# The sums of the MLP's first weight blocks move from VectorE to GpSimd

## The chip, the cores and the metric

The kernel runs on one core of one Trainium2 chip. The metric is device time in microseconds (us). The engines are named as in the profile: PE is TensorE, DVE is VectorE, ACT is ScalarE, POOL is GpSimd, SP is SyncE, which issues the loads.

## The reference

A two-layer decoder trunk over 512 positions of width 1024. Layer 0 mixes with a gated MLP over chunks and with latent attention, layer 1 with gated linear attention. Each layer ends with the same MLP of width 4096, and that is where the change lies:

```python
def sqrelu_mlp(x, w1, w2):
    return jnp.square(jax.nn.relu(x @ w1)) @ w2

x = layer_norm(ALPHA * x + y, ln1_g[layer], ln1_b[layer])
x = layer_norm(ALPHA * x + sqrelu_mlp(x, w_ff1[layer], w_ff2[layer]), ln2_g[layer], ln2_b[layer])
```

## The kernel before

All products are made in fp32 quality from three products of reduced precision: each operand is split into a high part (a cast on ACT, L164) and a low part, the operand less its high part (a subtraction on DVE, L165). For a weight block the parts are the tiles `whi` and `wlo`, for an activation `hh` and `hl`. PE multiplies high by high, high by low and low by high.

The MLP, `ff`, treats `x @ w1` in eight groups of columns. A group takes 256 columns of the left half of `w1` and 256 of the right half; together with the two halves of the rows that makes four blocks of 512 x 256: B11, B12, B21, B22. Group 0 is multiplied plainly. Groups 1 to 7 go by a Strassen-like scheme with seven products instead of eight, `P1, p5, p7, p6, p3, P2, p4` in this order (`LATER`, L506). These need seven weight blocks: B11, B21 and B22 as loaded, and four sums, made in place:

- t1 = B11 + B12 (over B11), used by p5
- t3 = B12 + B22 (over B12), used by p7
- t2 = t1 + B22 (over t1), used by p6
- t4 = t2 + B21 (over t2), used by p4

A sum may begin when both its inputs are there and when the block that it overwrites has been split. `SUM` (L353) holds this table.

The order of the weight blocks is the list `wseq`: in a group B11, t1, t3, t2, B22, B21, t4. Between groups stand the blocks of the second matrix, ("w2", chunk, half, row half). After group 0 come the w2 products of chunk 0, then groups 1 and 2 one behind the other, then chunk 1, group 3, chunk 2, group 4 and so on, so that groups 1 and 2 have no w2 products between them. `upto(n)` (L533) walks that list: it issues loads up to six blocks ahead and calls `terms1` (a block of `w1`) or `terms2` (a block of `w2`), each of which splits a block. It is called ahead of each product with the place of the block that the product needs, plus a few blocks of lead.

Three things set the order of work. PE and DVE run their instructions in the order in which the program writes them (`manual_schedule` for PE, `in_order` for DVE in the MLP). ACT, POOL and SP get an order from the framework's planner. Semaphores are put in by the framework wherever a tile is written and read by different engines.

Before the change `sum1` (L369) puts a sum on DVE (L374). `upto` calls it for the block about to be split and, one step early, for the next block in the list if that is a sum other than t1 (L543 to L546). So sums and low parts stand in one queue on DVE.

After a product, `product` (L455) joins accumulators and makes the squared ReLU: V and X (L489, L490), then the quarters C11, C22 (L477), C12 (L481), C21 (L485); each quarter goes through two ACT instructions (L428, L429), a cast to `hh` on ACT and a low part `hl` on DVE.

Raw blocks lie in the tiles `cr` (two buffers for B11 and B12 of one group) and `cr2` (one buffer with room for B22 and B21).

Of the kernel before, what the change touches and what calls it, by code (L numbers as in the profile page):

```python
# [17 lines left out]
ALU = mybir.AluOpType  # L18
# [85 lines left out]
def trunk(ctx: ExitStack, tc: tile.TileContext, a: dict, out: bass.AP):  # L104
    nc = tc.nc
# [57 lines left out]
    def split(hi, lo, src):  # L163
        nc.scalar.copy(hi, src)  # L164
        nc.vector.tensor_tensor(lo, src, hi.bitcast(F32), ALU.subtract)  # L165
# [19 lines left out]
    def tb(t):  # L185
        return slice(t * P, (t + 1) * P)
# [97 lines left out]
    def ff(layer, hp, fp, xp, out_proj, prefetch):  # L284

        w1, w2 = a["w_ff1"][layer], a["w_ff2"][layer]
# [64 lines left out]
        raws, got_w, kept2 = {}, {}, {}  # L351
        BLOCK = {"B11": (0, 0), "B12": (0, 1), "B22": (1, 1), "B21": (1, 0)}
        SUM = {"t1": ("B11", "B12"), "t3": ("B12", "B22"), "t2": ("t1", "B22"), "t4": ("t2", "B21")}  # L353

        def load1(g, n):

            for m in (n,) if g == 0 else {"B11": ("B11", "B12"), "B21": ("B21",), "t1": ("B22",)}.get(n, ()):
                if g == 0 and m != "B22":
                    raw = wp.tile([P, WG], F32, tag="raw", name="raw", bufs=3)
                elif g == 0 or m in ("B11", "B12"):  # L360
                    raw = xp.tile([P, WG], F32, tag="cr", name="cr", bufs=2)
                else:
                    if g not in kept2:
                        kept2[g] = xp.tile([P, 2, WG], F32, tag="xk", name="cr2")
                    raw = kept2[g][:, m == "B21"]
                raws[g, m] = raw
                nc.sync.dma_start(raw.rearrange("p (k c) -> p k c", k=HK_), w1v(*BLOCK[m], g))

        def sum1(g, n):  # L369

            if n in SUM and (g, n) not in raws:
                x, y = SUM[n]
                raws[g, n] = raws[g, x]
                nc.vector.tensor_tensor(raws[g, n], raws[g, x], raws[g, y], ALU.add)  # L374

        def pair(spare=None):

            if spare is not None:
                return [xp.tile([P, WG], F32R, tag=t, name="ws", **({"bufs": 2} if t == "cr" else {})) for t in spare]
            return wp.tile([P, WG], F32R, tag="whi", name="whi"), wp.tile([P, WG], F32R, tag="wlo", name="wlo")  # L380
# [3 lines left out]
        LAST = [("s4h", "s4l"), ("s3h", "s3l"), ("s2h", "s2l"), ("cr", "cr")]  # L384

        def terms1(g, n):
            sum1(g, n)
            raw = raws[g, n]
            if (g, n) == (0, "B22"):
                his = [hp.tile([P, HK_, P], F32R, tag="hh", name="wh") for _ in range(2)]  # L390
                los = [hp.tile([P, HK_, P], F32R, tag="hl", name="wl") for _ in range(2)]
                for j in range(2):
                    split(his[j], los[j], raw.rearrange("p (k c) -> p k c", k=HK_)[:, :, tb(j)])
            else:
                hi, lo = pair(EARLY[n] if g == 0 else None)
                split(hi, lo, raw)
                his, los = ([z.rearrange("p (k c) -> p k c", k=HK_)[:, :, tb(j)] for j in range(2)] for z in (hi, lo))
            got_w[g, n] = his, los

        def load2(c, n, half):  # L400
            r = half * 2048 + c * GF
            raw = wp.tile([P, WG], F32, tag="raw", name="raw", bufs=3)
            nc.sync.dma_start(raw.rearrange("p (k c) -> p k c", k=2),
                              w2[r:r + GF, n * 512:(n + 1) * 512].rearrange("(k p) c -> p k c", p=P))
            raws["w2", c, n, half] = raw

        def terms2(c, n, half):
            raw = raws.pop(("w2", c, n, half))
            hi, lo = pair(LAST[(c - NG + 2) * 2 + half] if c >= NG - 2 and n == 1 else None)
            split(hi, lo, raw)  # L410
            v = lambda x: x.rearrange("p (k c) -> p k c", k=2)
            got_w["w2", c, n, half] = v(hi), v(lo)
# [94 lines left out]
        slots, wseq = [], []  # L507
# [22 lines left out]
        at = {"load": 0, "terms": 0}  # L530
        LOADS, TERMS = 6, 6

        def upto(n, loads=None):  # L533

            while at["load"] < min(len(wseq), n + (LOADS if loads is None else loads)):
                w = wseq[at["load"]]
                at["load"] += 1
                (load2(*w[1:]) if w[0] == "w2" else load1(*w))
            while at["terms"] < min(len(wseq), n):
                w = wseq[at["terms"]]  # L540
                i = at["terms"]
                at["terms"] += 1
                if w[0] != "w2":  # L543
                    sum1(*w)
                if i + 1 < at["load"] and wseq[i + 1][1] in SUM and wseq[i + 1] != (w[0], "t1"):
                    sum1(*wseq[i + 1])  # L546
                (terms2(*w[1:]) if w[0] == "w2" else terms1(*w))

        todo = 0
        for _ in out_proj:  # L550
            todo += 1
            upto(min(todo, 4), 2)
        sums = x_sums()
        for n, (i, j, k) in enumerate(itertools.product(range(2), repeat=3)):
            upto(min(8, 4 + max(0, n - 1)))
            if n in (4, 5):
                next(sums)
            plain(i, j, k)
            if n == 1:
                x_T(NT - 1)  # L560
                x_lo(NT - 2)
                x_lo(NT - 1)
        for i, s in enumerate(slots):
            if s[0] == "w2":
                need = max(place["w2", s[1], s[2], 1], place["w2", s[1], s[2], 0])
                if s[1] == 0:
                    next(sums, None)
                    upto(max(need + 1, 8 + i // 2))
                else:
                    upto(min(need + 1 + TERMS, need + 1 + 2 * (s[3] + 1)))  # L570
                ff2_half(s[1], s[2], s[3])
                continue
            upto(place[s[0], PRODUCTS[s[1]][1]] + 1 + min(TERMS, 2 + s[0]))
            product(*s)
# [718 lines left out]
    with (tc.tile_pool(name="h0", bufs=8) as hp, tc.tile_pool(name="f0", bufs=2) as fp,  # L1293
          tc.tile_pool(name="x0", bufs=1) as xp, in_order()):
        v0 = ff(0, hp, fp, xp, steps, load_v0)
    with tc.tile_pool(name="m1", bufs=1) as mp:
        steps = out_proj_odd(odd_mixer(mp, v0))
    with (tc.tile_pool(name="h1", bufs=8) as hp, tc.tile_pool(name="f1", bufs=2) as fp,
          tc.tile_pool(name="x1", bufs=1) as xp, in_order()):
        ff(1, hp, fp, xp, steps, None)  # L1300
# [38 lines left out]
```

## Time and profile before

| | us |
|---|---|
| median of 3 runs | 1174.79 (1174.71 to 1175.62) |
| the profiled execution | 1176.24 |
| its span | 1174.2 |
| PE busy | 1146.1 (98%) |
| DVE busy | 825.3 (70%) |
| ACT busy | 520.3 (44%) |
| POOL busy | 4.6 (0%) |

The span is what the trace covers; 2.0 us of the profiled execution lie outside it. Matmuls overlap and their ends are modelled, so a busy PE is one that is not kept waiting. The MLP of layer 0 lies at about 231 to 550 us, that of layer 1 at about 822 to 1170 us.

### The profile page before, as it was taken

How to read it: one execution, taken by the hardware profiler on the slowest of the kernel's cores; microseconds unless marked ns; L12 is line 12 of the kernel's file. 1: busy time of each engine (PE TensorE's matmuls, PEld its weight loads, DVE VectorE, ACT ScalarE, POOL GpSimd, SP SyncE). 2: the span in 40 equal slices, each digit the busy share in tenths (PEclk: the TensorE clock that was granted, in tenths of full speed). 3: DMA queues.
4: the chain of work that ended last, by engine and by line, in shares of the span. 5: the costliest groups of instructions: out<-in, count | busy, mean ns of one | idle time of the engine just before them, and what ended most of it. 6: DMA issues, size and time to landing. Idle time of an engine off the chain costs nothing.

```text
span 1174.2 us, 17121 instructions
## 1 busy us (share of the span) xinstructions
PE 1146.1 (98%) x6888; PEld 999.5 (85%) x6888; DVE 825.3 (70%) x1562; ACT 520.3 (44%) x801; POOL 4.6 (0%) x13
## 2 busy tenths in 40 slices
PE   8999999999899999999999999999998999999997
PEld 8988788889888998997888888778998889889976
DVE  5745687785677567568758559898766866675665
ACT  5367462443644534443264433443536444445430
POOL 0000000000000000000000000000000000000000
PEclk9999999999999999999999999999999999999999
DMA  7413143132341332214235312221232333413121
GB/s 243 148 37 108 55 137 97 36 109 72 108 141 57 127 126 76 86 55 157 72 97 144 90 54 73 72 72 55 77 104 90 111 105 109 142 38 126 54 90 54
DMA packets 84206, 111.67 MB, mean 95 GB/s; under 512 B 6080, under 2 KB 53056, under 8 KB 84128
## 3 DMA queue, kind: packets, MB, share of 16 engines
q1 hardware_dynamic: 84128, 110.59, 29.6%
q8 instruction: 54, 0.88, 0.3%
q14 instruction: 24, 0.20, 0.1%
HBM read 108.47 MB, written 2.10 MB: 94 GB/s over the span
## 4 chain that ended last, share of the span: by engine, by line
PE 86%; DVE 7%; ACT 5%; issue 1%; DMA 0%; SPq 0%; DVEq 0%; ACTq 0%
PE f L443 24%; PE f L160 9%; PE f L161 9%; PE f L159 9%; PE vg L159 3%; PE vg L161 3%; PE vg L160 3%; PE op L159 3%; PE op L161 2%; PE op L160 2%; PE sc L822 1%; PE qk L159 1%; DVE wlo L165 1%; PE qk L160 1%; PE qk L161 1%; PE o L844 1%
## 5 line engine op out<-in xcount | busy, mean ns | idle before, releaser
L164 ACT CAST whi<-cr 128x1024 fp32r<-128x1024 f32 x98 | 99.9, 1047 | 179.4 <-DVE cr L374 116.8
L160 PE MATMUL f<-wlo,hh 128*128 128x512 f32 x448 | 177.0, 395 | 1.5 <-DVE wlo L165 1.5
L161 PE MATMUL f<-whi,hl 128*128 128x512 f32 x448 | 177.0, 395 | 0.5 <-DVE hl L165 0.5
L159 PE MATMUL f<-whi,hh 128*128 128x512 f32 x448 | 176.8, 395 | 0.0
L165 DVE TENSOR_TENSOR wlo<-cr,whi 128x1024 fp32r<-128x1024 f32 x98 | 118.8, 1219 | 15.0 <-ACT whi L164 14.9
L443 PE MATMUL f<-XH,wlo 128*128 128x256 f32 x448 | 126.1, 281 | 1.6 <-DVE wlo L165 1.6
L443 PE MATMUL f<-XH,whi 128*128 128x256 f32 x448 | 126.1, 281 | 0.8 <-ACT whi L164 0.8
L443 PE MATMUL f<-XL,whi 128*128 128x256 f32 x448 | 125.8, 281 | 0.0
L165 DVE TENSOR_TENSOR hl<-r,hh 128x512 fp32r<-128x512 f32 x64 | 44.2, 690 | 109.8 <-ACT hh L164 109.8
L160 PEld LDWEIGHTS f<-wlo,hh 128*128 128x128 f32 x448 | 84.3, 188 | 21.5 <-DVE wlo L165 2.4
L161 PEld LDWEIGHTS f<-whi,hl 128*128 128x128 f32 x448 | 84.3, 188 | 21.1 <-DVE hl L165 1.4
L159 PEld LDWEIGHTS f<-whi,hh 128*128 128x128 f32 x448 | 84.3, 188 | 19.2
L443 PE MATMUL f<-sh,wlo 128*128 128x256 f32 x336 | 96.2, 286 | 4.5 <-DVE wlo L165 4.5
L443 PE MATMUL f<-sh,whi 128*128 128x256 f32 x336 | 95.8, 285 | 0.0
L443 PE MATMUL f<-sl,whi 128*128 128x256 f32 x336 | 95.8, 285 | 0.0
L208 DVE SCALAR_TENSOR_TENSOR XN<-XN,f 128x512 f32<-128x512 f32 (+1 forms) x113 | 73.4, 676 | 20.1 <-PE f L161 20.1
L443 PEld LDWEIGHTS f<-XH,wlo 128*128 128x128 f32 x448 | 84.4, 188 | 2.0 <-DVE wlo L165 2.0
L443 PEld LDWEIGHTS f<-XH,whi 128*128 128x128 f32 x448 | 84.4, 188 | 1.8 <-ACT whi L164 1.2
L443 PEld LDWEIGHTS f<-XL,whi 128*128 128x128 f32 x448 | 84.4, 188 | 0.5
L164 ACT CAST whi<-raw 128x1024 fp32r<-128x1024 f32 x56 | 58.5, 1051 | 54.6 <-PE f L443 38.3
L137 ACT CAST whi<-raw 128x1024 fp32r<-128x1024 f32 (+3 forms) x61 | 60.2, 991 | 50.0 <-DMA raw<-in_w_in_odd 22.1
L138 DVE TENSOR_TENSOR wlo<-raw,whi 128x1024 fp32r<-128x1024 f32 (+3 forms) x61 | 69.9, 1151 | 15.2 <-ACT whi L137 15.0
(270 smaller groups left out, 2536.7 us busy)
## 6 DMA issues: line engine op xcount, KB each, us to landing
raw<-in_w_ff SPq DMA_DIRECT2D x70, 512.0 KB, 4.2
cr<-in_w_ff SPq DMA_DIRECT2D x58, 512.0 KB, 4.3
raw<-in_w_in_odd SPq DMA_DIRECT2D x24, 512.0 KB, 4.2
XN<-in_x SPq DMA_DIRECT2D x16, 256.0 KB, 3.3
raw<-in_w_in_even SPq DMA_DIRECT2D x8, 512.0 KB, 3.9
raw<-in_w_out_even SPq DMA_DIRECT2D x8, 512.0 KB, 3.7
raw<-in_w_out_odd SPq DMA_DIRECT2D x8, 512.0 KB, 3.5
LB<-in_ln_b SPq DMA_DIRECT2D x4, 512.0 KB, 4.3
```

The costliest lines, as they stand in the source:

```text
L137: nc.scalar.copy(hi[:, :n], raw[:, :n])
L138: nc.vector.tensor_tensor(lo[:, :n], raw[:, :n], hi[:, :n].bitcast(F32), ALU.subtract)
L159: nc.tensor.matmul(acc, lh, rh, start=first, stop=False)
L160: nc.tensor.matmul(acc, lh, rl, start=False, stop=False)
L161: nc.tensor.matmul(acc, ll, rh, start=False, stop=last)
L164: nc.scalar.copy(hi, src)
L165: nc.vector.tensor_tensor(lo, src, hi.bitcast(F32), ALU.subtract)
L208: nc.vector.scalar_tensor_tensor(x, x, ALPHA if first else 1.0, acc, ALU.mult, ALU.add)
L443: nc.tensor.matmul(d, l, r, start=first and j == k == i == 0, stop=j == 1 and k == HK_ - 1 and i == 2, skip_group_check=True)
L822: nc.tensor.matmul(sc[:, :N], qts[t][:B_QK, h, :], KT[:, h, :N], start=True, stop=True)
L844: nc.tensor.matmul(os[t][:, h, :], pT[:, j * P:(j + 1) * P], V[:, j, h, :], start=j == 0, stop=j == t)
```

## The change

`sum1` and its calls in `upto` go. In its place `sums1(g)` is called after each block of a group g > 0 has been split. It goes through the table of sums and issues, on POOL, each sum whose inputs have been loaded or made, if the block that it overwrites has been split (t3 is the exception: it overwrites B12, which is never split, and waits only for t1 to be issued, which reads B12). So t1 and t3 are written behind the split of B11, t2 behind that of t1, t4 behind that of t2.

```diff
-        def sum1(g, n):
-
-            if n in SUM and (g, n) not in raws:
-                x, y = SUM[n]
-                raws[g, n] = raws[g, x]
-                nc.vector.tensor_tensor(raws[g, n], raws[g, x], raws[g, y], ALU.add)
+        made = set()
+
+        def sums1(g):
+
+            for n, (x, y) in SUM.items():
+                if (g, n) not in raws and (g, x) in raws and (g, y) in raws and (n == "t3" or (g, x) in made):
+                    if n == "t3" and (g, "t1") not in raws:
+                        continue
+                    raws[g, n] = raws[g, x]
+                    nc.gpsimd.tensor_tensor(raws[g, n], raws[g, x], raws[g, y], ALU.add)
...
         def terms1(g, n):
-            sum1(g, n)
             raw = raws[g, n]
+            made.add((g, n))
...
             got_w[g, n] = his, los
+            if g:
+                sums1(g)
...
                 w = wseq[at["terms"]]
-                i = at["terms"]
                 at["terms"] += 1
-                if w[0] != "w2":
-                    sum1(*w)
-                if i + 1 < at["load"] and wseq[i + 1][1] in SUM and wseq[i + 1] != (w[0], "t1"):
-                    sum1(*wseq[i + 1])
                 (terms2(*w[1:]) if w[0] == "w2" else terms1(*w))
```

## Rows read from the trace of the kernel before

**Rows 1.** The page's first part: busy time, share of the span, instructions.

```profile
PE 1146.1 (98%) x6888; PEld 999.5 (85%) x6888; DVE 825.3 (70%) x1562; ACT 520.3 (44%) x801; POOL 4.6 (0%) x13
```

**Rows 2.** Windows: length, busy time of each engine, PEclk (granted clock), DMA share.

```profile
302.00:304.00 2.00, 0.12 (x1) 0.12 (x2) 2.00 (x3) 0.00 (x0) 0.00 (x0) 1.00 0.00 0
304.00:306.00 2.00, 2.00 (x12) 2.00 (x13) 2.00 (x2) 0.00 (x0) 0.00 (x0) 0.62 0.00 0
306.00:308.00 2.00, 2.00 (x12) 2.00 (x12) 2.00 (x3) 1.88 (x2) 0.00 (x0) 0.52 0.00 0
...
340.00:382.00 42.00, 42.00 (x265) 37.81 (x264) 30.37 (x35) 19.81 (x25) 0.00 (x0) 1.00 0.31 101
```

**Rows 3.** Timeline of PE: start, length, instruction; in brackets the wait before it.

```profile
294.33 0.39 PE L443 MATMUL f<-XH,whi 128*128 128x256 f32 x1 [0.42 <-ACT whi L164]
295.64 0.39 PE L443 MATMUL f<-XH,wlo 128*128 128x256 f32 x1 [0.81 <-DVE wlo L165]
303.88 0.39 PE L443 MATMUL f<-sh,wlo 128*128 128x256 f32 x1 [2.25 <-DVE wlo L165]
...
330.36 0.50 PE L160 MATMUL f<-wlo,hh 128*128 128x512 f32 x1 [0.73 <-DVE wlo L165]
...
895.27 0.58 PE L443 MATMUL f<-sh,wlo 128*128 128x256 f32 x1 [2.26 <-DVE wlo L165]
```

**Rows 4.** Timeline of DVE around group 2 of layer 0.

```profile
287.35 1.22 DVE L165 TENSOR_TENSOR wlo<-cr,whi 128x1024 fp32r<-128x1024 f32 x1
...
291.37 0.69 DVE L165 TENSOR_TENSOR hl<-r,hh 128x512 fp32r<-128x512 f32 x1 [2.19 <-ACT hh L164]
291.98 1.22 DVE L374 TENSOR_TENSOR cr<-cr 128x1024 f32<-128x1024 f32 x1
293.23 1.23 DVE L374 TENSOR_TENSOR cr<-cr,cr 128x1024 f32<-128x1024 f32 x1
294.37 1.22 DVE L165 TENSOR_TENSOR wlo<-cr,whi 128x1024 fp32r<-128x1024 f32 x1
...
297.24 1.22 DVE L165 TENSOR_TENSOR wlo<-cr,whi 128x1024 fp32r<-128x1024 f32 x1
298.38 0.69 DVE L485 TENSOR_TENSOR f<-f,LG 128x512 f32<-128x512 f32 x1
302.00 0.69 DVE L165 TENSOR_TENSOR hl<-r,hh 128x512 fp32r<-128x512 f32 x1 [2.93 <-ACT hh L164]
302.61 2.35 DVE L165 TENSOR_TENSOR wlo<-cr,whi 128x1024 fp32r<-128x1024 f32 x2
...
326.74 0.69 DVE L165 TENSOR_TENSOR hl<-r,hh 128x512 fp32r<-128x512 f32 x1 [1.98 <-ACT hh L164]
```

**Rows 5.** Timeline of ACT in the same stretch.

```profile
290.71 1.14 ACT L164 CAST hh<-r 128x512 fp32r<-128x512 f32 x2
293.23 1.05 ACT L164 CAST whi<-cr 128x1024 fp32r<-128x1024 f32 x1 [1.37 <-DVE cr L374]
...
297.36 2.00 ACT L164 CAST whi<-cr 128x1024 fp32r<-128x1024 f32 x2 [1.66 <-DVE cr L374]
...
299.75 1.04 ACT L164 CAST whi<-cr 128x1024 fp32r<-128x1024 f32 x1
```

**Rows 6.** Groups by line: the larger group of sums (count, busy us, mean ns).

```profile
L374 DVE TENSOR_TENSOR cr<-cr,cr 128x1024 f32<-128x1024 f32 x42 | 51.1, 1217 | 0.1
```

**Rows 7.** Timelines of POOL and DVE, 25 to 30 us.

```profile
25.16 0.40 POOL L777 COPY kn<-kr 128x256 f32<-128x256 f32 x1 [24.65 <-DVE ny L182]
27.98 0.68 POOL L896 TENSOR_SCALAR_AFFINE_SELECT ws<-ws 128x512 f32<-128x512 f32 x1 [2.42 <-DMA ws<-in_a_w_s]
...
25.87 0.94 DVE L138 TENSOR_TENSOR wlo<-raw,whi 128x768 fp32r<-128x768 f32 x1
...
28.27 1.20 DVE L138 TENSOR_TENSOR wlo<-raw,whi 128x768 fp32r<-128x768 f32 x1
```

**Rows 8.** Timeline of SP's queue, 277 to 286 us: loads of blocks of `w1`.

```profile
277.68 0.92 SPq L367 DMA_DIRECT2D cr<-in_w_ff  x2
```

## The prediction

> **What bounds the kernel now.** I read the busy shares first, then TensorE's waits, then the granted clock in slices of 2 us around the longest wait, then the queues of VectorE (DVE) and ScalarE (ACT) in order of time. TensorE is busy 98% of the span, DVE 70%, GpSimd (POOL) 0% [rows 1]. So DVE's 825 us are not the bound, and taking work off DVE pays only where TensorE stands still for it. In the steady part of the MLP it never does: from 340 to 382 us TensorE is busy for all 42 us and DVE for 30 [rows 2]. What is left are a few gaps. In layer 0 the product p5 of group 2 waits 0.42 us for the high part of its block t1 and 0.81 us for the low part, p6 of group 2 waits 2.25 us for the low part of t2, and the first w2 product that needs block (1, 1, 1) waits 0.73 us; the second layer repeats them (2.26 us for the long one) [rows 3]. After the 2.25 us gap the granted clock reads 0.62 and 0.52 for two slices of 2 us, where it was 1.00 before; the 1.23 us of the two gaps before it cost no clock [rows 2, 3]. 0.62 and 0.52 of 2.4 GHz lie between its two levels, so most of these 4 us ran at 1.2 GHz: (0.38 + 0.48) x 2 = 1.7 us lost. Shorter gaps at the close of a layer lie behind group 7, where no sum is left to make, and stay.
>
> That gives a ceiling: 0.42 + 0.81 + 2.25 + 0.73 + 1.7 = 5.9 us a layer, 11.8 us for both. The change cannot bring more than about 1%.
>
> **Why the long gap is there.** Groups 1 and 2 follow each other with no w2 products between them, so DVE must prepare seven blocks while TensorE uses seven. Its queue there, in the written order [rows 4]: low part of B11 (287.35), a wait for ACT until hl at 291.37, the sums t1 and t3 of group 2 (291.98, 293.23), low t1 (294.37), a sum, low t3 (297.24), the subtraction of C21 (298.38), 2.93 us of waiting for ACT, hl (302.00), low t2 (302.61). TensorE resumes 1.27 us after the start of the last, at 303.88. ACT's side [rows 5]: the cast of t1 waits 1.37 us for its sum, that of t2 1.66 us, and a cast slips into the chain of C21: the same chain without one makes DVE wait 1.98 us (326.74) instead of 2.93 [rows 4].
>
> **The change, part by part.** *Removed from DVE:* 2 layers x 7 groups x 4 = 56 sums of 1.217 us (42 of them in one group of rows), 68.2 us [rows 6]. Hidden behind TensorE everywhere but in the gaps above, so worth nothing by itself.
>
> *Added to POOL:* 56 sums of 128x1024 f32. No row shows this operation. The nearest are a copy of 256 columns (0.40 us) and a select over 512 columns (0.68 us), each with one input [rows 7]. Their difference gives 0.28 us for 256 columns, 1.09 ns a column, and 0.12 us fixed. A sum reads two inputs: 0.12 + 1024 x 1.09 ns = 1.2 us if the second input is free (as on DVE, 1.22 us), 2.35 us if each column is paid twice. An engine that takes 0.40 us for 256 copied columns is no faster with more inputs, so I take the upper end, 2.4 us, and keep 1.2 to 4.5 us for the range. In a sentence by itself: the Trainium skill, GPSIMD Engine Reference, section 3.1, has 4497 ns for a sum of 2048 columns; half of that, 2.25 us, would give the same sum within 0.2 us.
>
> *Beside it, DVE loses time.* Two subtractions of 128x768 with both inputs in SBUF stand in the trace, one that began after the copy had ended (0.94 us) and one of which 0.39 us lay beside the select (28.27 to 28.66): it took 1.20 us [rows 7]. So 0.26 of 0.39 us were lost, two thirds of the time shared. All low parts (`wlo`, `hl`) are of this kind; the subtractions that read PSUM I take as free. One case only, and with a one-input operation: I keep zero and full loss as the ends and take two thirds. The Trainium skill's GPSIMD Engine Reference, section 1, says the same kind of thing, that the engine shares its SBUF interfaces with VectorE and conflicts with instructions of two SBUF inputs; the row agrees (0.26 us lost), and what it would make of the time is the second rival.
>
> *Order and queues.* POOL's queue holds nothing else in the MLP. A group's sums stand in it as t1, t3, t2, t4; t3 needs the load of B22 and would hold t2 back if that came late. No DMA is moved; the load of a next block still waits for the low parts that read the old one. What is new is that ACT's cast waits for POOL, not for DVE; behind that cast stand the casts and Relu's of the other group, and behind them DVE's low parts in written order.
>
> *The stretch again, group 2 of layer 0.* Low B11 ends at 288.5 as before. POOL makes t1 from 288.6 to 291.0, t3 to 293.4. ACT's two casts `hh` end at 291.85, then its cast of t1 takes 1.05 us, to 292.9 (it began at 293.23 before). hl (291.37) loses 0.4 us beside t3, low t1 starts at 292.9, loses 0.3 and ends at 294.4. TensorE reaches p5 at 293.9 and needs the low part two matmuls later: a gap of some 0.3 instead of 1.23 us. POOL makes t2 from 294.4 to 296.8. The other hl (0.61 us) loses 0.4 beside it and ends at 295.4. Low t3 then has 1.4 us beside t2, does 0.47 of its 1.13 us in that time and the rest by 297.5; it ended at 298.38. From there it is C21's chain as before: in the trace TensorE resumed 298.38 + 5.50 = 303.88; without the cast inside the chain it is 2.93 - 1.98 = 0.95 shorter. So TensorE resumes between 297.5 + 4.55 = 302.05 and 297.5 + 5.50 = 303.0. Which of the two is ACT's order, which no line of the kernel writes; I take the middle, 302.5: **1.4 us gained**, between 0.9 and 1.8.
>
> *The clock.* From 295.64 to 301.63 TensorE took 6.0 us to get from the second gap to the long one; now it starts at 294.4, loses some 0.3 at t3, and arrives at 300.7. The new gap is 1.4 to 2.3 us, against 2.25 that cost clock and 1.23 that did not. I take half of the 1.7 us, **0.9**, between 0 and 1.7.
>
> *The 0.73 us gap.* One sum (t1 of group 3, 1.13 us) leaves DVE's queue ahead of that block, but POOL then makes t1 and t3 of group 3 just there, beside an hl and the low part waited for: (0.61 + 1.13) us of work could lose more than the sum gave. I take 0, between +0.7 and -1.0, and a loss of 0.2 for t4, whose sum now starts only when low t2 is done.
>
> Sum: 1.4 + 0.9 - 0.2 = 2.1 us a layer, **4.2 us**. The rows are those of an execution of 1176.24 us (span 1174.2); the median is 1174.79, 1.45 less, and the gaps do not depend on that: 1174.79 - 4.2 = **1170.6 us**.
>
> **The rivals.** *Quiet neighbours.* DVE loses next to nothing, ACT casts early, the clock stays: 0.9 us of the first gap, 2.2 of the second, 1.7 of clock, 0.5 of the last make some 5 us a layer: 1164.5 us. For it: the memory traffic of one sum is small beside what one select row tells; against it: that row.
>
> *What leaves DVE comes back.* Two thirds of 2.4 us is 1.6 us lost per sum where DVE has low parts to make all the time, more than the 1.13 us removed. Then low t3 ends no earlier than 298, the cast stays inside C21's chain, the clock falls: 0 to 1 us a layer, 1173 to 1175 us, within 0.2% (2.35 us, about what a measurement of this kernel can tell from no change). The Trainium skill, Perfetto Trace Analysis, section Optimizing Scalar/DVE Operations, warns of just that: moving work between those two might not help because they share a read port. For it: the select row; against it: between 288 and 302 DVE waits for ACT 2.19 and 2.93 us [rows 4], and in those pauses POOL disturbs nobody.
>
> *POOL is the new chain (slower).* t1 and t3 stand one behind the other, and low t3 waits for both and a cast: 288.6 + 2d + 1.1 + 1.1 for a sum of d us, then the chain of 4.55 to 5.50. Without losses TensorE resumes at 303.88 if d is 4.0 to 4.3 us, and with 1 us lost beside t2 if it is 3.5. A sum of 4.5 us puts low t3 at 299.8 to 300.8 and costs 1 to 2 us a layer at p6 and about 1 at the last gap: 1179 us. For it: no row shows a POOL operation with two inputs, and DVE slows it too; against: it needs twice the price of the rows.
>
> *It does not do what it says* only if POOL's sums are held back by a load: t3 by B22. The last loads of group 2 were issued by 278.6 us, 12 us before POOL would reach t3 [rows 8], so I give that nothing of its own.
>
> **How the numbers follow.** My forecast 0.40 (1168 to 1172.4), quiet neighbours 0.17, what leaves comes back 0.26, POOL as the chain 0.17. So faster by over 0.2% 0.57, within 0.2% 0.26, slower 0.17. The range reaches from the quiet case, 1164.5, to 1177.0, which cuts off the dearer half of the slow case.
>
> **What would show it.** 56 sums on POOL of about 2.4 us; low parts beside them at 1.5 to 2 us instead of 1.22; ACT's cast of t1 in group 2 at about 292 us; TensorE's gap at p5 under 0.5 us and at p6 under 2.3; no gap at all in groups 3 to 7; the clock after p6's gap tells half of the term. Sums of over 3.5 us, or low parts of over 2.5 us, make it wrong upwards; low parts unchanged make it wrong downwards.

## The result, and the profile after

The changed kernel takes 1191.66 us (1190.88 to 1193.12), the kernel before, on the same chip, 1175.2 us (1174.71 to 1176.21). The ratio is 1.014 with an interval of 1.0123 to 1.0158: slower by 16.5 us. The forecast was 1170.6 us in a range of 1164.5 to 1177.0, so it had the sign wrong. The profiled span of after is 1190.0 us, against 1174.2.

The low parts of the blocks in `cr` in the kernel before, then the page of after: busy time and three groups of instructions (count, busy us, mean ns, then idle time before them and what ended it):

```profile
L165 DVE TENSOR_TENSOR wlo<-cr,whi 128x1024 fp32r<-128x1024 f32 x98 | 118.8, 1219 | 15.0 <-ACT whi L164 14.9
...
PE 1149.9 (97%) x6888; PEld 1001.7 (84%) x6888; DVE 795.7 (67%) x1506; ACT 518.2 (44%) x801; POOL 152.5 (13%) x69
...
L165 DVE TENSOR_TENSOR wlo<-cr,whi 128x1024 fp32r<-128x1024 f32 x98 | 148.0, 1525 | 2.5 <-ACT whi L164 1.9
...
L378 POOL TENSOR_TENSOR cr<-cr,cr 128x1024 f32<-128x1024 f32 x42 | 107.6, 2563 | 160.5 <-DVE wlo L165 81.5
L378 POOL TENSOR_TENSOR cr<-cr 128x1024 f32<-128x1024 f32 x14 | 39.6, 2830 | 507.6 <-DVE wlo L165 350.4
```

The 56 sums stand on POOL. They took 68.2 us of DVE [rows 6], so DVE's 825.3 us [rows 1] should have fallen to 757.1. They fell to 795.7: 38.6 us came back, most of it as low parts that grew longer. The 98 low parts of blocks in `cr` alone went from 118.8 to 148.0 us, from 1219 to 1525 ns in the mean.

The timeline of PE in after, the gaps of the MLP of layer 0 (in brackets the wait before the instruction), and two of layer 1:

```profile
296.59 0.39 PE L449 MATMUL f<-XH,wlo 128*128 128x256 f32 x1 [3.02 <-DVE wlo L165]
305.93 0.39 PE L449 MATMUL f<-sh,wlo 128*128 128x256 f32 x1 [1.82 <-DVE wlo L165]
314.93 0.36 PE L449 MATMUL f<-XH,whi 128*128 128x256 f32 x1 [0.43 <-DVE r L483]
334.73 0.50 PE L160 MATMUL f<-wlo,hh 128*128 128x512 f32 x1 [3.94 <-DVE wlo L165]
375.94 0.50 PE L159 MATMUL f<-whi,hh 128*128 128x512 f32 x1 [1.58 <-ACT r L434]
461.25 0.50 PE L159 MATMUL f<-whi,hh 128*128 128x512 f32 x1 [0.64 <-ACT r L434]
...
897.33 0.39 PE L449 MATMUL f<-XH,wlo 128*128 128x256 f32 x1 [3.01 <-DVE wlo L165]
934.68 0.50 PE L160 MATMUL f<-wlo,hh 128*128 128x512 f32 x1 [3.09 <-DVE wlo L165]
```

These answer to [rows 3]. The p5 gap grew from 0.42 + 0.81 to 3.02 us. The p6 gap shrank from 2.25 to 1.82. The gap at the w2 product grew from 0.73 to 3.94, and gaps of 0.43, 1.58 and 0.64 us are new, the last two in groups where there were none. Layer 0 has 11.4 us of gaps instead of 4.2, layer 1 has 9.1.

The clock, in windows (length, busy times, then PEclk, DMA share, GB/s):

```profile
298.00:300.00 2.00, 2.00 (x11) 2.00 (x10) 2.00 (x1) 0.59 (x1) 1.37 (x1) 0.50 0.04 8
...
306.00:308.00 2.00, 2.00 (x17) 2.00 (x18) 2.00 (x2) 0.00 (x0) 2.00 (x1) 1.00 0.00 0
...
336.00:338.00 2.00, 2.00 (x7) 1.54 (x6) 2.00 (x2) 0.00 (x0) 2.00 (x1) 0.50 0.64 243
```

After the 3.02 us and the 3.94 us gap the clock stood at 0.50, the lower of its two levels, for a window, and between the levels in the windows beside it (0.90 and 0.74, 0.79 and 0.86): 1.7 us lost each time. After the 1.82 us gap it stayed at 1.00. Before there was one such fall a layer [rows 2], now there are two. In layer 0 that makes 7.2 us of gaps and 1.7 of clock. Layer 1 of before has the same four gaps as its layer 0 (0.42, 0.81, 2.26 and 0.77 us), so layer 1 adds 4.8 and 1.7. Together that is 15.4 of the 15.8 us by which the span grew: nearly the whole loss is in these few places.

The largest of them, in the queues. ACT in after:

```profile
290.63 1.05 ACT L164 CAST whi<-cr 128x1024 fp32r<-128x1024 f32 x1 [1.19 <-POOL cr L378]
291.59 0.62 ACT L435 ACTIVATE r<-r 128x512 f32<-128x512 f32 x1
293.11 1.05 ACT L164 CAST whi<-cr 128x1024 fp32r<-128x1024 f32 x1 [0.90 <-POOL cr L378]
294.06 1.13 ACT L164 CAST hh<-r 128x512 fp32r<-128x512 f32 x2
```

POOL in after (the first three of the stretch, then two sums and a select from other places):

```profile
288.20 2.40 POOL L378 TENSOR_TENSOR cr<-cr 128x1024 f32<-128x1024 f32 x1 [12.36 <-DVE wlo L165]
290.68 2.40 POOL L378 TENSOR_TENSOR cr<-cr,cr 128x1024 f32<-128x1024 f32 x1
296.68 2.69 POOL L378 TENSOR_TENSOR cr<-cr,cr 128x1024 f32<-128x1024 f32 x1 [3.60 <-DVE wlo L165]
...
340.74 2.40 POOL L378 TENSOR_TENSOR cr<-cr,cr 128x1024 f32<-128x1024 f32 x1 [2.42 <-DVE wlo L165]
427.23 2.41 POOL L378 TENSOR_TENSOR cr<-cr,cr 128x1024 f32<-128x1024 f32 x1 [6.94 <-issue]
...
27.63 1.44 POOL L897 TENSOR_SCALAR_AFFINE_SELECT ws<-ws 128x512 f32<-128x512 f32 x1 [2.72 <-DMA ws<-in_a_w_s]
```

DVE in after, at the same places:

```profile
287.98 0.69 DVE L487 TENSOR_TENSOR f<-LB,f 128x512 f32<-128x512 f32 x1
294.71 0.69 DVE L165 TENSOR_TENSOR hl<-r,hh 128x512 fp32r<-128x512 f32 x1 [6.04 <-ACT hh L164]
295.32 1.22 DVE L165 TENSOR_TENSOR wlo<-cr,whi 128x1024 fp32r<-128x1024 f32 x1
296.45 0.68 DVE L165 TENSOR_TENSOR hl<-r,hh 128x512 fp32r<-128x512 f32 x1
297.06 3.40 DVE L165 TENSOR_TENSOR wlo<-cr,whi 128x1024 fp32r<-128x1024 f32 x1
...
332.25 0.69 DVE L165 TENSOR_TENSOR hl<-r,hh 128x512 fp32r<-128x512 f32 x1 [6.05 <-ACT hh L164]
...
342.37 1.86 DVE L165 TENSOR_TENSOR wlo<-cr,whi 128x1024 fp32r<-128x1024 f32 x1
428.46 2.27 DVE L165 TENSOR_TENSOR wlo<-cr,whi 128x1024 fp32r<-128x1024 f32 x1
...
27.61 0.95 DVE L138 TENSOR_TENSOR wlo<-raw,whi 128x768 fp32r<-128x768 f32 x1
```

Two things can be seen. First, POOL makes t1 in 2.40 us and has it ready at 290.60, and ACT casts it at 290.63, 2.6 us earlier than before [rows 5]. But the planner has put the casts of t1 and t3 ahead of the cast `hh` of a quarter. In between ACT stands still for POOL (1.19 and 0.90 us), and `hh` comes at 294.06 instead of 290.71 [rows 5]. DVE's next instruction in written order is `hl`, which needs that cast. So DVE stands idle for 6.04 us, with low t1, whose cast was done at 291.7, queued behind `hl`, and starts it at 295.32. PE resumes 1.27 us later. The same happens ahead of the w2 product: DVE waits 6.05 us for `hh` until 332.25, where it waited 1.98 [rows 4].

Second, low t3 starts at 297.06, while a sum runs on POOL (296.68 to 299.37), and takes 3.40 us instead of 1.22. It lost 2.18 us, and the sum had 2.31 us to run when it started. The same at 428.46: 1.18 us of the sum left, 1.05 lost; at 342.37: 0.77 left, 0.64 lost.

### The profile page after: what moved, and what is told of

Same layout as the page of the kernel before. It is cut to its first block, busy times and chain, and to the rows that moved or that the text cites. A ratio compares the mean times of both kernels' runs of the same rounds, so it can differ in the third digit from the quotient of the medians.

```text
span 1190.0 us, 17217 instructions
## 1 busy us (share of the span) xinstructions
PE 1149.9 (97%) x6888; PEld 1001.7 (84%) x6888; DVE 795.7 (67%) x1506; ACT 518.2 (44%) x801; POOL 152.5 (13%) x69
## 5 line engine op out<-in xcount | busy, mean ns | idle before, releaser
L165 DVE TENSOR_TENSOR hl<-r,hh 128x512 fp32r<-128x512 f32 x64 | 44.2, 691 | 167.3 <-ACT hh L164 167.3
L165 DVE TENSOR_TENSOR wlo<-cr,whi 128x1024 fp32r<-128x1024 f32 x98 | 148.0, 1525 | 2.5 <-ACT whi L164 1.9
L378 POOL TENSOR_TENSOR cr<-cr,cr 128x1024 f32<-128x1024 f32 x42 | 107.6, 2563 | 160.5 <-DVE wlo L165 81.5
L378 POOL TENSOR_TENSOR cr<-cr 128x1024 f32<-128x1024 f32 x14 | 39.6, 2830 | 507.6 <-DVE wlo L165 350.4
```

Source lines behind the costliest of these rows:

```text
L378: nc.gpsimd.tensor_tensor(raws[g, n], raws[g, x], raws[g, y], ALU.add)
```

## The experiments

I started from two theories. *ACT's queue* (theory A in the expectations): the planner's order, with casts that wait for POOL ahead of `hh`, is what costs. *Shared memory access* (theory B): low parts stand still beside a sum. Two more came in with later runs: *place*, that a sum issued early is bad by itself, and *lateness* (theory C), that a sum which is slow to come is. The edits below are against the changed kernel unless another is named. The ratio given is to the kernel before, run in the same job.

**The changed kernel with ACT in written order (e1).** `in_order` covers ACT too, so `hh` and the casts come as the program writes them:

```diff
-        return tc.manual_schedule(engines={mybir.EngineType.DVE})
+        return tc.manual_schedule(engines={mybir.EngineType.DVE, mybir.EngineType.Activation})
```

> The changed kernel, with ACT in the MLP bound to the order in which the program writes its instructions, as DVE already is; the orders of all other engines are the same. Theory A (order on ACT): the 16 us were lost because the planner put ACT's casts of t1 and t3 ahead of the casts hh of a quarter and ahead of Relu's, so that ACT stood waiting for POOL while DVE waited 6 us for hh. Then here DVE's two waits of 6 us for hh in a layer go back to about 2 to 3 us, TensorE's gaps of 3.0 us (p5) and 3.9 us (w2) fall under 1 us, and the time is 1168 to 1178 us. Theory B (shared time on DVE): low parts beside sums take 3.4 instead of 1.2 us whatever ACT's order is; then the time stays at 1186 to 1192 us. Read against the kernel before with the same order on ACT, since that order may cost something by itself.

Measured: 1184.84 us against 1175.14, ratio 1.0089 (1.0069 to 1.011). It gave back over a third of the loss, less than theory A wanted and more than theory B allowed. POOL's second sum, DVE's timeline and the group of `hl`:

```profile
290.04 2.41 POOL L378 TENSOR_TENSOR cr<-cr,cr 128x1024 f32<-128x1024 f32 x1
...
290.06 2.92 DVE L165 TENSOR_TENSOR hl<-r,hh 128x512 fp32r<-128x512 f32 x1 [1.98 <-ACT hh L164]
...
294.65 3.41 DVE L165 TENSOR_TENSOR wlo<-cr,whi 128x1024 fp32r<-128x1024 f32 x1
...
L165 DVE TENSOR_TENSOR hl<-r,hh 128x512 fp32r<-128x512 f32 x64 | 70.0, 1094 | 99.7 <-ACT hh L164 99.7
```

The wait for `hh` is back at 1.98 us. In its place `hl` itself now takes 2.92 instead of 0.69 us: it runs into the second sum (290.04 to 292.45). Over the kernel the 64 `hl` grew from 44.2 to 70.0 us. So the stall has a second cause, which the first had hidden: while DVE waited for `hh`, POOL's two sums disturbed nobody. PE's longest gaps in layer 0 are 1.53 us at p5, 1.90 in group 3 and 2.95 at the w2 product, and only the last of them is followed by a fall of the clock.

**The kernel before with ACT in written order (e2)**, the same edit.

> The kernel before (sums on DVE), with ACT in the MLP bound to the written order. It prices that order alone. Both theories: within 1172 to 1180 us. In this order the cast of t2 stands behind the chain of C21, so DVE's wait of 2.93 us before hl should read about 2 us.

Measured: 1174.12 us against 1175.14, ratio 0.9996 (0.9987 to 1.0005). The written order is worth nothing by itself: it moves PE's waits about (5.7 us of gaps in the MLP of layer 0 against 5.0, but no fall of the clock behind them), and the time is the same. It counts where ACT's casts wait for POOL.

**The sums in the new places, but on DVE (e3).**

```diff
+                    if n == "t3" and g == 1 and (g, "t1") not in made:
+                        continue
                     raws[g, n] = raws[g, x]
-                    nc.gpsimd.tensor_tensor(raws[g, n], raws[g, x], raws[g, y], ALU.add)
+                    nc.vector.tensor_tensor(raws[g, n], raws[g, x], raws[g, y], ALU.add)
```

> The changed kernel with the sums on DVE: only the place of the sums changes, behind the split that frees their block (t3 of group 1 later, behind t1's split, since its load waits for DVE). If the place were at fault it would be over 1180 us. Theories A and B both put the loss on POOL, so here it is gone: t1 and t3 of group 2 are made in the 2.2 us in which DVE waited for ACT anyway, the gaps at p5 vanish (1.2 us a layer) and the one at p6 shrinks: 1166 to 1173 us.

Measured: 1180.18 us against 1175.14, ratio 1.0046 (1.0028 to 1.0064): a miss, since I had expected a gain. DVE and ACT in that kernel:

```profile
287.24 1.23 DVE L380 TENSOR_TENSOR cr<-cr 128x1024 f32<-128x1024 f32 x1
288.50 1.22 DVE L380 TENSOR_TENSOR cr<-cr,cr 128x1024 f32<-128x1024 f32 x1
289.64 0.69 DVE L489 TENSOR_TENSOR f<-LB,f 128x512 f32<-128x512 f32 x1
```

```profile
289.75 1.05 ACT L164 CAST whi<-cr 128x1024 fp32r<-128x1024 f32 x1 [0.21 <-DVE cr L380]
290.70 0.59 ACT L436 ACTIVATE r<-f 128x512 f32<-128x512 f32 x1
```

Made as soon as they can be, t1 and t3 stand on DVE ahead of the subtraction that opens C12, and their casts ahead of its Relu. The quarter is late, and PE waits 1.75 us at p5, 1.76 at p6 and 2.49 at the w2 product of layer 0. So issuing a sum as soon as its parts are there costs even without POOL: work that nobody needs yet stands ahead of work that somebody does.

**The kernel before, with sums on POOL that nobody waits for (e4).** Behind the splits of B11, t1 and t2, sums of 128 columns of the low part into a small tile, eight for one of the changed kernel's. The order of DVE and ACT does not change:

```diff
+            for _ in range({"B11": 2, "t1": 1, "t2": 1}.get(n, 0) if g else 0):
+                noise = xp.tile([P, P], F32, tag="noise", name="noise", bufs=1)
+                for j in range(WG // P):
+                    x = lo.bitcast(F32)[:, tb(j)]
+                    nc.gpsimd.tensor_tensor(noise, x, x, ALU.add)
```

> The kernel before, all sums on DVE, every engine's order unchanged; POOL makes, behind the same four splits of a group, an unused sum of 1024 columns (eight pieces of 128 columns from a low part into a small tile). Nobody waits for them; they only share SBUF with DVE. Theory B (shared time): low parts and sums on DVE beside them take two to three times as long, and as DVE has more to do than in the changed kernel, at least as much is lost: 1183 to 1195 us. Theory A: the low parts slow down just so, but most of it falls into DVE's pauses: 1176 to 1182 us.

Measured: 1178.85 us against 1175.14, ratio 1.0033 (1.002 to 1.0046). The pieces took 742 ns in the mean, 0.40 us where nothing held them up, and DVE's busy time grew from 825.3 [rows 1] to 852.2 us. In the trace no instruction waits for these pieces, so POOL's reads alone slow DVE and cost 3.7 us. That is below what theory B had put here (1183 to 1195 us) and inside theory A's range. POOL was busy longer than in the changed kernel (337 us against 152) and in short pieces, so this is no measure of the size.

**ACT in written order, and the sums cut to 64 of 1024 columns (e5)** (against the first experiment; the other columns stay unsummed):

```diff
-                    nc.gpsimd.tensor_tensor(raws[g, n], raws[g, x], raws[g, y], ALU.add)
+                    nc.gpsimd.tensor_tensor(raws[g, n][:, :64], raws[g, x][:, :64], raws[g, y][:, :64], ALU.add)
```

> As e1 (sums on POOL, ACT in the written order, every engine's order the same), but each sum covers 64 of its 1024 columns; the other columns of the four blocks stay unsummed. So a sum is there almost at once and hardly shares SBUF with DVE. e1 took 10.7 us more than e2, which has the sums on DVE in the same order of ACT. If these 10.7 us come from the sums on POOL themselves, by their lateness or by the time shared with DVE, they are gone here, and with them DVE's 68 us of sums: 1166 to 1173 us. If it stays above 1180 us, the cause is none of the two but the waits between the engines.

Measured: 1164.89 us against 1172.63, ratio 0.9934 (0.992 to 0.9949). With a sum that is nearly free, the gaps that the prediction named go, but for some 0.47 and 0.75 us at p6 in each layer, and no fall of the clock comes behind them. The gain, 7.7 us, is two thirds of what I had called the ceiling. It doesn't tell whether a sum costs by being late or by standing in DVE's way.

**The same, made late by fills (e6)** (against e5, only 64 columns summed). POOL fills a small tile, which only writes, between a short sum and the block. The fills and the first piece ran ahead of what they should have followed, so the block came only 0.3 to 0.4 us late.

```diff
-                    nc.gpsimd.tensor_tensor(raws[g, n][:, :64], raws[g, x][:, :64], raws[g, y][:, :64], ALU.add)
+                    late = xp.tile([P, P], F32, tag="late", name="late", bufs=1)
+                    nc.gpsimd.tensor_tensor(late[:, :64], raws[g, x][:, :64], raws[g, y][:, :64], ALU.add)
+                    for _ in range(4):
+                        nc.gpsimd.memset(late, 0.0)
+                    nc.gpsimd.tensor_tensor(raws[g, n][:, :64], raws[g, x][:, :64], late[:, :64], ALU.add)
```

> As e5, but each short sum is held back on POOL by four fills of a small tile between a first and a last piece of 64 columns, some 2 to 3 us in all, about as long as a whole sum. Fills only write, and a fill cost a subtraction beside it nothing (1.22 us at 715 us of the kernel before). So the results come as late as in e1, but DVE is left alone. Theory C (lateness): ACT's casts and DVE's low parts wait as in e1, 1180 to 1186 us. Theory B (shared time on DVE): the sum may be late, there is slack for that; low parts take 1.22 us and the time is 1167 to 1175 us.

Measured: 1165.67 us against 1172.63, ratio 0.9935 (0.9919 to 0.9952). It differs from the one above by nothing, and says nothing about lateness. The next two mend it.

**Late, and held (e9)** (against the first experiment, two pieces of 64 columns are made, the rest stays unsummed). The first 64 columns of the block are written at once, so the chain cannot run ahead; the last piece comes behind six fills:

```diff
-                    nc.gpsimd.tensor_tensor(raws[g, n], raws[g, x], raws[g, y], ALU.add)
+                    late = xp.tile([P, P], F32, tag="late", name="late", bufs=1)
+                    c, d = slice(0, 64), slice(64, 128)
+                    nc.gpsimd.tensor_tensor(raws[g, n][:, c], raws[g, x][:, c], raws[g, y][:, c], ALU.add)
+                    nc.gpsimd.tensor_tensor(late[:, c], raws[g, n][:, c], raws[g, n][:, c], ALU.add)
+                    for _ in range(6):
+                        nc.gpsimd.memset(late, 0.0)
+                    nc.gpsimd.tensor_tensor(raws[g, n][:, d], raws[g, y][:, d], late[:, c], ALU.add)
```

> e6 did not hold the sums back: its first piece and its fills ran ahead of the wait, and only 0.3 us stood behind it. Here the first piece of 64 columns writes the block itself, so it waits for the split, and a second small sum, six fills and a last piece follow in a chain, 2.4 to 3 us as the whole sum in e1. 896 of 1024 columns stay unsummed. ACT and DVE have the order of e1. Theory C (lateness): casts and low parts wait as in e1, 1179 to 1186 us. Theory B (shared time on DVE): hl and low parts keep 0.69 and 1.22 us and the time stays at 1165 to 1171 us.

Measured: 1175.48 us against 1174.71, ratio 1.001 (1.0 to 1.0019), between theories B and C. POOL in that kernel, first and last piece of t1:

```profile
288.25 0.32 POOL L380 TENSOR_TENSOR cr<-cr 128x64 f32<-128x64 f32 x1 [8.71 <-DVE wlo L165]
...
290.77 0.86 POOL L384 TENSOR_TENSOR cr<-cr,late 128x64 f32<-128x64 f32 x1
```

This block, t1 of group 2, is held for 3.4 us, and t2 for 2.8; in e1 it was 2.4 and 2.8. So nothing comes earlier here than with whole sums. The low parts are hardly slowed (`hl` 704 ns, `wlo` 1227 ns in the mean). It takes all the gain, but does not bring the loss: 1.001 against 1.0089 with whole sums.

**The same with two fills (e10)**, so that t1 and t2 of group 2 are held for 1.8 and 1.6 us. That is shorter than the sum that it stands for, in spite of the label:

```diff
-                    for _ in range(6):
+                    for _ in range(2):
```

> e9 held its sums 3.4 us, a whole sum takes 2.4. Here two fills in place of six, so that the result comes 2.3 to 2.5 us after the split, as in e1; 896 of 1024 columns stay unsummed; ACT and DVE in the order of e1. e9 was 0.1% over the kernel before, e5 (no delay) 0.7% under it, e1 0.9% over it. Theory B (shared time on DVE) leaves nothing for a delay of this length: 1164 to 1169 us. Theory C (lateness): at least half of e9's loss, 1170 to 1175 us. What then lies between here and e1 is the time shared.

Measured: 1170.15 us against 1173.48, ratio 0.9969 (0.9956 to 0.9982), between e5 and e9, at the lower end of what theory C allowed. The groups of low parts:

```profile
L165 DVE TENSOR_TENSOR wlo<-cr,whi 128x1024 fp32r<-128x1024 f32 x98 | 119.2, 1229 | 54.7 <-ACT whi L164 54.7
...
L165 DVE TENSOR_TENSOR hl<-r,hh 128x512 fp32r<-128x512 f32 x64 | 44.5, 695 | 104.3 <-ACT hh L164 104.3
```

**The same with ACT's order left to the planner (e11).** DVE's and ACT's instructions then stand in the order of the changed kernel, one by one:

```diff
-        return tc.manual_schedule(engines={mybir.EngineType.DVE, mybir.EngineType.Activation})
+        return tc.manual_schedule(engines={mybir.EngineType.DVE})
```

> e10 with ACT's order left to the planner; it comes out the same as in the changed kernel, instruction by instruction, and so does DVE's. So this is the changed kernel with sums that come as late but leave DVE alone (896 of 1024 columns stay unsummed). Theory A (order on ACT): casts of t1 and t3 still stand ahead of hh, DVE waits about 6 us for hh and TensorE 2 to 3 us at p5 and at the w2 product: 1176 to 1184 us. If sharing is all, it is within 2 us of e10.

Measured: 1178.32 us against 1173.48, ratio 1.0042 (1.0027 to 1.0057), inside theory A's range. DVE in that kernel, one of POOL's pieces of t2, and PE at p6:

```profile
291.78 0.69 DVE L165 TENSOR_TENSOR hl<-r,hh 128x512 fp32r<-128x512 f32 x1 [4.41 <-ACT hh L164]
292.39 1.22 DVE L165 TENSOR_TENSOR wlo<-cr,whi 128x1024 fp32r<-128x1024 f32 x1
...
301.22 0.69 DVE L165 TENSOR_TENSOR hl<-r,hh 128x512 fp32r<-128x512 f32 x1 [5.14 <-ACT hh L164]
...
294.47 1.16 POOL L381 TENSOR_TENSOR late<-cr 128x64 f32<-128x64 f32 x1
...
303.10 0.58 PE L455 MATMUL f<-sh,wlo 128*128 128x256 f32 x1 [3.47 <-DVE wlo L165]
```

The low parts keep their length (690 and 1227 ns in the mean), but DVE waits 4.41 and 5.14 us for `hh`, and PE 1.38 us at p5 and 3.47 at p6. This is the price of the queue with DVE left alone, though not quite with equal sums: t2 was held 2.8 us here and 1.6 in e10, because two of its pieces stood still beside low parts (0.64 and 1.16 us instead of some 0.3). And the gap at the w2 product, which theory A had put at 2 to 3 us, is 0.53 us in layer 0 and 1.53 in layer 1: there the order alone cost little.

These last ones and the first make a table of ratios to before (held: t1 and t2 of group 2, from their split to the last piece):

| | ACT as written | ACT by the planner |
|---|---|---|
| sums of 64 columns | 0.9934 | not run |
| held by two fills (1.8 and 1.6 us; by the planner 1.8 and 2.8), low parts unslowed | 0.9969 | 1.0042 |
| held by six fills (3.4 and 2.8 us), low parts unslowed | 1.001 | not run |
| whole sums of 2.4 us | 1.0089 | 1.014 (the change) |

Down the first column, lateness costs 0.4% with two fills and 0.8% with six. The step to whole sums costs 0.8% more than blocks held for as long or longer, and 1.2% more than blocks held for less. So the shared access is worth between 9 and 14 us. Across, ACT's order costs 0.73% without slowed low parts (8.6 us, some of it by the later t2) and 0.51% with them (6 us). The intervals leave some 3 us of room on each of these. From the nearly free sums (0.9934) to the change (1.014) it is 24 us in all: the 16.5 us lost and the gain that did not come.

**Sums on DVE, put into its pauses (e7).** If DVE's waits for `hh` are the only idle place, the free sums belong there. Against the kernel before: from group 2 on, t1, t3 and t2 are issued on DVE between the cast `hh` and its `hl`, when their inputs are there (`fill1`).

```diff
+        def fill1():
+            for g in range(2, NG):
+                for n in ("t1", "t3", "t2"):
+                    x, y = SUM[n]
+                    if (g, n) not in raws and (g, y) in raws and ((g, "t1") in raws if n == "t3" else (g, x) in made):
+                        sum1(g, n)
...
-            split(f(hh), f(hl), r)
+            nc.scalar.copy(f(hh), r)
+            fill1()
+            nc.vector.tensor_tensor(f(hl), r, f(hh).bitcast(F32), ALU.subtract)
```

> The kernel before, sums on DVE, with one change: from group 2 on a sum whose block is free is written between a quarter's subtraction and its hl, where DVE waits some 2 us for ACT's chain anyway. If the gaps of TensorE in group 2 come from sums that stand in front of low parts in DVE's queue, the gap at p5 goes (1.2 us a layer), t2 comes 1 to 2 us earlier, and with a gap at p6 under 2 us the clock may hold: 1166 to 1172 us. If ACT's order takes the casts of these sums ahead of hh as in the changed kernel: 1174 to 1182 us.

Measured: 1167.58 us against 1172.63, ratio 0.9958 (0.9942 to 0.9974), faster than both kernels. DVE there:

```profile
287.54 1.22 DVE L374 TENSOR_TENSOR cr<-cr 128x1024 f32<-128x1024 f32 x1
288.79 1.23 DVE L374 TENSOR_TENSOR cr<-cr,cr 128x1024 f32<-128x1024 f32 x1
290.63 0.69 DVE L443 TENSOR_TENSOR hl<-r,hh 128x512 fp32r<-128x512 f32 x1 [0.61 <-ACT hh L441]
```

Two sums now stand in the pause where DVE had waited 2.19 us before `hl` [rows 4], and 0.61 us of it are left. The p5 gaps are gone, and p6 waits 1.76 us, with a fall of the clock behind it.

**The same with ACT in written order (e8).**

> e7 with ACT in the written order, to be read against e2 (1174.1). The casts of the early sums cannot go ahead of hh here, so the sums fill DVE's pauses at no cost: gaps of 0.3 to 0.8 us in group 2 and of 1.5 us at the w2 product shrink: 1167 to 1173 us. If it is no faster than e2, those gaps are ACT's own, not DVE's.

Measured: 1168.85 us against 1172.63, ratio 0.9963 (0.9948 to 0.9978): not to be told from the one above. It is faster than e2, which has the same order on ACT (0.9996), so the gaps that went were DVE's and not ACT's own.

## Why the prediction was wrong

*What bounds the kernel, and the ceiling.* Right in the main. Nearly all that was lost lies in a few gaps and in the clock behind them, most of it in the gaps that were named; 2.65 us of the gaps of layer 0 (0.43, 1.58 and 0.64) came at places that were not. With nearly free sums the ratio is 0.9934, or 7.7 us, inside the 11.8 us of the ceiling; no run came nearer to it.

*The price of a sum.* Right: 2.40 us forecast, 2.40 us for the two sums that open the stretch, and 2.56 and 2.83 in the mean of the two groups, since DVE held some sums up. t1 was to be ready at 291.0 and was at 290.6. The rival in which POOL is the new chain comes nearest in time (1179 us), but for a reason that did not occur: it needed sums of 3.5 us or more there. (Its lower end of 4.0 us should have been 3.8: 303.88 less 5.50 less 290.8, halved.)

*"ACT's two casts `hh` end at 291.85, then its cast of t1."* This is the first step that failed. It took ACT's order from the trace of before and moved one cast along it. ACT's order is not written, and the planner made another one for the changed kernel, with the casts of t1 and t3 ahead of both `hh`. I had noted that ACT would wait for POOL and that the other group's casts, and DVE's low parts behind them, stand in that queue, and gave it no price. It cost a wait of 6.04 us on DVE. By the held sums with and without the written order, and the whole sums with and without it, it is worth 6 to 8.6 of the 24 us between nearly free sums and the change. Why the planner chose so is not settled. That the calls stand at other places in the program is not the reason: a program with `sum1` at its old places and only its engine changed, which was built but not timed, has the same order on every engine as the changed kernel. So the new places of the calls changed nothing by themselves.

*"Two thirds of the time shared."* The second step that failed, a term read wrongly from a right row. A low part that starts beside a running sum loses nearly all that is left of the sum: 2.18 of 2.31, 1.05 of 1.18, 0.64 of 0.77 us, and 2.23 of 2.39 in the first experiment. Each time 0.13 to 0.16 us are not lost. The select row had 0.39 us left and lost 0.26, which is the same 0.13 less [rows 7]. Read as a proportion it gave two thirds; read as a stop with a fixed allowance it would have given over 90% for a sum of six times the length. The end "full loss" of that term was nearly the right value, and the low part of 3.40 us lies beyond the 2.5 us that I had named as the point from which the prediction is wrong. That the instruction that starts second is the one that stops shows on the other side too: in after the select started 0.02 us after the low part and took 1.44 instead of 0.68 us, while the low part took its usual 0.95. The Trainium skill, SBUF — State Buffer, section Who interferes with whom, says that a VectorE instruction with two SBUF inputs contends with a GpSimd instruction that reads SBUF and not with one that only writes it, that the ports which the two engines share are an exclusive lock, and that the order of issue decides who blocks. The traces agree: the second one stood still in either order (3.40 us beside a sum, 1.44 us for the select), and the kernel with two fills left the low parts at 695 and 1229 ns.

*The 0.73 us gap at zero, "no gap at all in groups 3 to 7".* Wrong: 3.94, 1.58 and 0.64 us. The first is ACT's queue again, with DVE's wait of 6.05 us, but it takes the length of whole sums too: with the same order and sums held for less the gap was 0.53 us in layer 0 and 1.53 in layer 1 (e11), and in the first experiment it is still 2.95 us, now from a slowed `hl`. The two others are matmuls that wait for a Relu on ACT to free their accumulator, and at the first of them that Relu stood behind two casts that waited for POOL:

```profile
371.00 1.05 ACT L164 CAST whi<-cr 128x1024 fp32r<-128x1024 f32 x1 [4.23 <-POOL cr L378]
374.35 1.04 ACT L164 CAST whi<-cr 128x1024 fp32r<-128x1024 f32 x1 [2.29 <-POOL cr L378]
```

The prediction looked at one stretch, costed it in detail and took the other by a sentence; it cost more than the first.

*The clock.* The size was right, 1.7 us a fall. There are two falls a layer instead of the half of one that I took, one of them at a place where none was expected. The p6 gap did become shorter (1.82 us) and no fall came behind it; that this was for its length is not shown (see the last section).

*PE's resumption at p6, forecast 1.4 us earlier.* The gap itself, 1.82 us, lies in the 1.4 to 2.3 us that were forecast. But PE came to it late from p5, and it resumed at 305.93 instead of 302.5 (303.88 before): low t3, forecast to end at 297.5, started only at 297.06 and lost 2.18 us instead of 0.9.

The decomposition leaves some room. The shares of ACT's order and of the slowed low parts depend on each other (while DVE waits for `hh`, sums disturb nobody), and the held blocks were not exactly as late as a whole sum. Both causes are shown by runs, and lateness as a third and smaller one; their exact shares are not.

## What to carry to other kernels

A producer moved to a slower engine must be followed in every queue that reads it: the reader's engine may be ordered so that it waits ahead of unrelated work, and then the price is that work's delay, not the producer's length. The sums moved from VectorE to GpSimd did not run beside VectorE's subtractions of two SBUF inputs; they took turns with them. For such a move, count what is left of the instruction that started first against the one that starts second, whichever engine it is on. Where VectorE's load is only a problem of place, look first for its own pauses: here the same sums, put into the waits for ScalarE, gave 0.42%, and moved away they cost 1.4%.

## What the runs showed of the hardware

The stop beside a running POOL sum is close to complete and did not depend on the length of what is stopped: `hl` of 0.69 us and `wlo` of 1.22 us lost the same 2.2 us. A DVE instruction with one input in PSUM was not slowed (`f<-f,LG` took 0.68 us at 371.98 in after, while a sum had 2.3 us left to run). POOL loses less often: 42 of its 56 sums stayed at 2.4 us, and 12 of the others, at 2.7 to 3.3, started while a low part was running. One sum in each layer took 5.05 us, held behind five DVE instructions of 0.69 us in a row.

A gap's length alone did not decide whether the clock fell from its upper level (1.00 in the windows) to its lower one (0.50). It fell behind gaps of 1.76 us (e7), 2.25 [rows 2, 3], 2.95 (e1), 3.02, 3.47 (e11) and 3.94 us, and stayed at 1.00 behind 1.82 us in after, 1.90 in e1 and 2.49 at the w2 product of layer 0 in e3. What came just before the gap does not decide it either. In e4 both layers have the same gaps in the same order (0.62, 1.10, 0.38 and then 2.37 us at p6, to within 0.01), and only layer 1 lost clock behind them:

```profile
306.00:308.00 2.00, 2.00 (x19) 2.00 (x18) 2.00 (x3) 0.17 (x1) 1.92 (x2) 1.00 0.00 0
...
898.00:900.00 2.00, 2.00 (x12) 2.00 (x13) 2.00 (x2) 0.00 (x0) 1.84 (x3) 0.62 0.00 0
```

In e3 it was the same with the gap of 1.75 us at p5 of the two layers. What decides was not found, so a forecast of a single fall of this kind is a guess.
